# Decay tiles of an SSM loaded by one plain transfer and clamped on ScalarE, begun half a group earlier, in a hybrid attention and SSM block

## The chip, the core and the metric

The kernel runs on one core of a Trainium2 chip. The metric is the device time of one execution in microseconds; the time of a kernel is the median of its runs. The profile is taken from one further execution, whose own time stands beside its span below.

## What is computed

One layer on x (256 tokens by 2048 channels, float32): a normalised u = rms_norm(x) goes through one wide projection `w_in`; one part feeds sparse attention with an indexer, one part a Mamba-2 mixer; gates merge the two; then comes a SwiGLU channel mixer. The change touches the Mamba part, of which this is the core, and the sum over its groups:

```python
a = dt * a_head                                  # negative, per token and head
acum = cumsum(a)
decay = exp(where(causal, acum[t] - acum[s], -inf))
cb = einsum('btgn,bsgn->btsg', c, b)             # 8 groups g, state 128
y = einsum('btsg,btsgh,bsghp->btghp', cb, decay, xc)   # 8 heads h of 64 in a group
...
y = (y + d_skip * xs) * silu(z)
yg = y * rsqrt(mean(y * y) + eps) * g_norm       # mean within a group
y_ssm = sum over groups of yg @ w_ssm_branch     # 512 channels of a group each
```

The reference does this in steps of 64 tokens with a carried state. The kernel computes the whole 256 by 256 causal matrix of each head at once.

## The kernel before

Everything on the tensor engine (PE) is fp32 accuracy made of fp32r products. Weights come from memory in chunks of 1 MB, tiles `raw`, three buffers, issued on the SP queue (L415). ScalarE (ACT) rounds half a chunk to `hi` (L427), VectorE (DVE) takes the rest `lo` (L429), and PE makes three products (L489). Five pairs of `hi` and `lo` may be in flight. Some chunks are "sevens" (L440 to L455): seven block products in place of eight, for which DVE first builds the tiles `ts` from `raw` (L444, L450, L451). DVE, POOL and SP are put in order by a scheduler; the order of PE and ACT is set by hand: jobs are generators that yield a pause (a count of matmuls of the main stream, and a kind such as FREES or LATER), and between two chunk steps the jobs whose pause is over add their next piece.

The SSM stage is the loop over 8 groups at L910. For group g, `mixed()` makes 8 chunks of projection (the group's x and z, 256 by 512 each), `finish(pend...)` runs the job of group g-1 up to its result, `job_of(ssm_steps(g, ...))` starts the job of this group, and `ssm_out(g-1)` makes four chunks of `w_ssm_branch` products for the group before: its results leave PSUM through ACT as tiles `sums`, scaled by `rsg` (L900), and POOL's DMA adds them to `acc_d` in memory (L905, an accumulating transfer; 512 KB each, four per group).

The job `ssm_steps` (L803) runs beside those chunks:

- Two decay tiles `E` of 4 heads (128 by 4 by 384) are loaded by POOL: first the mask, broadcast over heads (L810), then `acum_d` (the cumulative sums, in memory), added onto it by an accumulating broadcast transfer (L812), which waits until the mask has landed.
- `cps` = C Bᵀ on PE (L819, L820), copied to `cbm` by ACT (L822).
- `conv_steps` (L727): transposes (L739), a first tap by ACT (L743), three more by DVE (L750), and one Silu of 1024 columns (L754), which waits for the job `decay_steps` (`behind`, L752).
- `decay_steps` (L789): per head two Exp with a bias per partition, 256 and 128 columns (L796); per pair of heads one DVE product with `cbm` (L800).
- Silu of z (L828); x transposed back (L835) and scaled by dt on DVE into `xdt` (L836).
- The products `yp` = xdt by E (L848), on DVE the skip (L854); z transposed (L865), product on DVE (L867), split `yh`, `yl` (L870, L873), square and sum (L878 to L886), and on POOL the small chain of the reciprocal root `rsg` (L142 to L153).

After the groups the accumulated `acc_d` is read back as two tiles `acc` of 1 MB (L960) for the attention stage, which works in four steps of 512 columns (`attn_steps`, L965).

Of the kernel before, what the change touches and what calls it, by code (L numbers as in the profile page):

```python
# [8 lines left out]
F32 = mybir.dt.float32  # L9
# [53 lines left out]
K_ID = 0  # L63
K_T = 128
K_CA = 128
K_SA = 256
K_CI = 384
K_SI = 448
K_V0 = 512
K_V1 = 640  # L70
K_N = 896


@with_exitstack
def hybrid_block(ctx, tc, xt, x, consts, mask, cols, heads, gfin, w_a, w_i, w_m, w_g, w_ab, w_sb, w_o, w_f1, w_f2, out):
    nc = tc.nc
# [51 lines left out]
    headp = cp.tile([SH, 2], F32, name="headp")  # L128
    ident = kc[:, K_ID : K_ID + P]
    neg_half = cp.tile([P, T], F32, name="neg_half")  # L130
    nc.gpsimd.memset(neg_half, -0.5)
# [143 lines left out]

    wz = cp.tile([P, 512], mybir.dt.bfloat16, name="wz")
    nc.vector.memset(wz, 0.0)
    for i in range(9):
# [317 lines left out]
    def head_steps():  # L596
# [68 lines left out]
        nc.vector.tensor_scalar(rest, dl[:, P:S], dl[:, P - 1 : P], None, ALU.add)  # L665
        nc.vector.tensor_scalar(r2, dl, -1.0, None, ALU.mult)
        nc.gpsimd.dma_start(acum_d[:, 0:P], dl[:, 0:P])
# [16 lines left out]
        tp = tr_t([P, 4, SH])  # L684
        for i, src in enumerate((r1[:, 0:P], r1[:, P:S], r2[:, 0:P], r2[:, P:S])):
            nc.tensor.transpose(tp[:, i, :], src, ident[:SH, :SH])
# [45 lines left out]
    def conv_steps(xk, cb, dst, behind=None, gap=12):  # L732

        for h in range(2):
            tp = tr_t([P, 2, S])
            for c in range(2):
                for t in range(T):
                    o = (2 * h + c) * P
                    nc.tensor.transpose(tp[:, c, t * P : (t + 1) * P], xk[t][:, o : o + P], ident)  # L739
            k = 2 * h  # L740
            for c in range(2):
                ch = cb * 4 + k + c
                nc.scalar.activation(dst[:, k + c, :], tp[:, c, :], AF.Identity, scale=ccol(C_CW, 3 * 48 + ch), bias=ccol(C_CB, ch))  # L743
# [7 lines left out]
            yield (6, FREES) if h else gap  # L751
# [32 lines left out]

    first_e = paced(v[0][0])

    acc_d = dp.tile([S, D], F32, name="acc_d")

    def decay_steps(g, Es, cbm):  # L789

        yield (6, LATER)
        for q in range(2):
            for hh in range(4):
                h = g * HPG + 4 * q + hh
                for i, e in ((2, Es[q][:, hh, 0:S]), (3, Es[q][:, hh, S:384])):
                    nc.scalar.activation(e, e, AF.Exp, bias=dcols[:, i, h : h + 1])  # L796
                yield (9, LATER)
                if hh % 2:
                    e = Es[q][:, hh - 1 : hh + 1, :]
                    nc.vector.tensor_tensor(e, e, cbm.unsqueeze(1).broadcast_to([P, 2, 384]), ALU.mult)  # L800
                    yield (3, LATER)

    def ssm_steps(g, xk, z, res):  # L803
        scaled(xk)
        Es = []
        for q in range(2):
            E = big_t([P, 4, 384], name="E")
            Es.append(E)
            with tc.issue_after(paced(xk[0]) if q else first_e) if g == 0 else nullcontext():
                nc.gpsimd.dma_start(E, mask.unsqueeze(1).broadcast_to([P, 4, 384]))  # L810
            h = g * HPG + 4 * q
            nc.gpsimd.dma_start(  # L812
                E.rearrange("p h s -> p (h s)"),
                acum_d[h : h + 4, :].rearrange("h s -> (h s)").partition_broadcast(P),
                accum_op=ALU.add,
            )
        yield 6
# [3 lines left out]
        cbm = smx.tile([P, 384], F32, tag="cbm", bufs=1, name=nm("cbm"))  # L821
        nc.scalar.activation(cbm, cps, AF.Copy)  # L822
        yield 6
        xs = mid_t([P, 4, S], name="xsc")
        decayed = job_of(decay_steps(g, Es, cbm))
        yield from conv_steps(xk, g, xs, decayed, 12 if g else 24)
        for t in range(T):
            nc.scalar.activation(z[t], z[t], AF.Silu, scale=rs(t))  # L828
        yield 12
        xdt = mid_t([P, T, 512], name="xdt")  # L830
        hs = slice(g * HPG, (g + 1) * HPG)
        for t in range(T):
# [6 lines left out]
            )  # L839
            yield 18 if t else 12  # L840
        for q in range(2):
            yp = sd_t([P, 2, S], name="yp")
# [9 lines left out]
            for m in range(2):  # L852
# [513 lines left out]
def _layout(inp):  # L1366
# [33 lines left out]
    a["consts"] = cst  # L1400
    future = np.where(np.triu(np.ones((P, P), np.float32)) > 0, 0.0, NEG_BIAS).astype(np.float32)
    a["mask"] = np.ascontiguousarray(np.concatenate([future, np.zeros((P, P), np.float32), future], axis=1))

    a["cols"] = np.ascontiguousarray(np.concatenate([
# [64 lines left out]
```

## Time and profile before

| | us |
|---|---|
| median of 3 runs | 1996.97 (1993.53 to 1997.56) |
| the profiled execution, its own time | 1997.86 |
| its span in the profile | 1995.8 |
| PE busy | 1952.8 (98%) |
| DVE busy | 1604.6 (80%) |
| ACT busy | 1177.9 (59%) |
| POOL busy | 93.2 (5%) |

The span is the time from the first to the last instruction of the profiled execution. Busy times are sums over instructions; matmuls overlap in the pipeline, so the share of PE contains some of its short waits. The mean clock granted to PE over the span was 0.994 of full speed. The SSM groups 1 to 7 lie between 230 and 860 us. There the queue of SP moved most of its bytes as weight chunks, and the queue of POOL the `sums`, the masks and `acum_d`.

### The profile page before, as it was taken

What the parts mean: (1) busy time and instruction counts of PE and PEld (TensorE: products, weight loads), DVE (VectorE), ACT (ScalarE), POOL (GpSimd) and SP (SyncE); (2) the same over time, 40 slices, a digit from 0 to 9 for tenths busy, and PEclk for the clock granted to TensorE, in tenths of its full rate; (3) what the DMA queues carried; (4) which work ended last, traced back from release to release, by engine and by line L of the source; (5) the groups of instructions that cost most, each with busy time, mean ns of one, the idle gap of its engine ahead of it and who ended that gap; (6) DMA issues with size and microseconds to landing.
All of it is one profiled execution on the core that took longest, in us unless ns stands there. A gap on an engine that the chain in (4) does not pass through costs nothing.

```text
span 1995.8 us, 23976 instructions
## 1 busy us (share of the span) xinstructions
PE 1952.8 (98%) x8990; PEld 1600.0 (80%) x8990; DVE 1604.6 (80%) x2109; ACT 1177.9 (59%) x1564; POOL 93.2 (5%) x149
## 2 busy tenths in 40 slices
PE   9999999899999999999999999999999999999998
PEld 7889787677777877778888888788888888888886
DVE  6878978777777778688998565789989999889864
ACT  6666475665765765556666445565655566555553
POOL 0000010110210210100000000000000000000000
PEclk9999999999999999999999999999999999999999
DMA  8566765957867866854455555455654655555553
GB/s 325 179 214 213 239 223 186 280 187 228 260 198 246 258 206 202 251 193 169 171 191 185 200 196 181 146 205 198 216 198 179 213 199 203 213 196 211 194 207 127
DMA packets 63908, 413.45 MB, mean 207 GB/s; under 512 B 7296, under 2 KB 7808, under 8 KB 20656
## 3 DMA queue, kind: packets, MB, share of 16 engines
q1 hardware_dynamic: 51120, 360.86, 50.1%
q0 software_dynamic: 11152, 47.29, 10.2%
q10 hardware_dynamic: 1520, 3.78, 0.5%
q8 instruction: 70, 1.15, 0.2%
q14 instruction: 46, 0.38, 0.1%
HBM read 392.93 MB, written 18.97 MB: 206 GB/s over the span
## 4 chain that ended last, share of the span: by engine, by line
PE 79%; DVE 9%; DMA 6%; ACT 4%; issue 2%; POOL 0%; SPq 0%; DVEq 0%; ACTq 0%; POOLq 0%
PE p L1199 31%; PE mm L489 29%; DMA raw<-in_w_m_dram 5%; PE mm L169 4%; PE mm L170 4%; PE mm L168 4%; DVE lo L429 4%; PE p L489 2%; ACT hi L427 1%; PE yp L848 1%; PE lg L979 1%; PE tr L1237 0%; DVE xsc L750 0%; DVE E L800 0%; DVE xb L530 0%
## 5 line engine op out<-in xcount | busy, mean ns | idle before, releaser
L489 PE MATMUL mm<-hi,ua 128*128 128x512 f32 (+1 forms) x1920 | 563.4, 394 | 2.6 <-DVE xb L530 1.5
L427 ACT ACTIVATE hi<-raw 128x1024 fp32r<-128x1024 f32 (+1 forms) x352 | 349.4, 1008 | 266.0 <-PE mm L489 161.0
L429 DVE TENSOR_TENSOR lo<-raw,hi 128x1024 fp32r<-128x1024 f32 (+1 forms) x352 | 403.5, 1161 | 120.4 <-ACT hi L427 119.7
L489 PEld LDWEIGHTS mm<-hi,ua 128*128 128x128 f32 x1920 | 354.0, 189 | 72.9 <-issue 3.0
L1121 ACT ACTIVATE hi<-raw 128x1024 fp32r<-128x1024 f32 x240 | 233.3, 979 | 132.2 <-PE p L1199 99.9
L1199 PE MATMUL p<-hi,opa 128*128 128x512 f32 x924 | 306.0, 390 | 1.5 <-ACT opf L1086 1.5
L489 PE MATMUL mm<-lo,ua 128*128 128x512 f32 (+1 forms) x960 | 301.0, 389 | 0.0
L1122 DVE TENSOR_TENSOR lo<-raw,hi 128x1024 fp32r<-128x1024 f32 x240 | 265.1, 1120 | 8.2 <-ACT hi L1121 7.4
L489 PEld LDWEIGHTS mm<-lo,ua 128*128 128x128 f32 x960 | 181.1, 189 | 37.3 <-DVE lo L429 0.3
L1199 PEld LDWEIGHTS p<-hi,opa 128*128 128x128 f32 x924 | 173.5, 188 | 37.6 <-ACT opf L1086 2.0
L200 DVE TENSOR_TENSOR lo<-raw,hi 128x1024 fp32r<-128x1024 f32 (+2 forms) x97 | 115.1, 1194 | 85.3 <-ACT hi L199 85.2
L1199 PE MATMUL p<-lo,opa 128*128 128x512 f32 x462 | 180.2, 391 | 0.0
L199 ACT ACTIVATE hi<-raw 128x1024 fp32r<-128x1024 f32 (+2 forms) x97 | 99.6, 1035 | 110.2 <-PE mm L170 98.4
L1199 PE MATMUL p<-hi,act 128*128 128x512 f32 x416 | 133.1, 390 | 0.0
L1199 PE MATMUL p<-hi,opb 128*128 128x512 f32 x352 | 126.9, 390 | 0.0
L1199 PEld LDWEIGHTS p<-lo,opa 128*128 128x128 f32 x462 | 86.7, 188 | 17.9 <-DVE lo L1122 0.2
L1121 ACT ACTIVATE hi<-tb 128x1024 fp32r<-128x1024 f32 x45 | 47.8, 1062 | 87.6 <-PE p L1199 45.1
L427 ACT ACTIVATE hi<-ts 128x1024 fp32r<-128x1024 f32 (+1 forms) x64 | 65.7, 1042 | 45.8 <-DVE ts L451 24.9
L1199 PEld LDWEIGHTS p<-hi,act 128*128 128x128 f32 x416 | 78.1, 188 | 16.3
L489 PE MATMUL mm<-hi,yh 128*128 128x512 f32 x256 | 86.4, 410 | 3.6 <-ACT sums L900 2.7
L1199 PE MATMUL p<-lo,act 128*128 128x512 f32 x208 | 80.5, 390 | 0.0
L489 PE MATMUL mm<-lo,yh 128*128 128x512 f32 x256 | 79.5, 391 | 0.0
(335 smaller groups left out, 3232.8 us busy)
## 6 DMA issues: line engine op xcount, KB each, us to landing
raw<-in_w_f_dram SPq DMA_DIRECT2D x132, 1024.0 KB, 4.8
raw<-in_w_m_dram SPq DMA_DIRECT2D x120, 1024.0 KB, 5.4
raw<-in_w_sb_dram SPq DMA_DIRECT2D x32, 1024.0 KB, 5.0
acc_d<-sums POOLq DMA_DIRECT2D x32, 512.0 KB, 10.0
raw<-in_w_g_dram SPq DMA_DIRECT2D x16, 1024.0 KB, 4.8
raw<-in_w_ab_dram SPq DMA_DIRECT2D x16, 1024.0 KB, 4.8
raw<-in_w_o_dram SPq DMA_DIRECT2D x16, 1024.0 KB, 4.8
E<-in_mask_dram POOLq DMA_DIRECT2D x16, 768.0 KB, 9.6
```

Source lines behind the costliest of these rows:

```text
L168: nc.tensor.matmul(o, lh, rh, start=(kt == 0), stop=False)
L169: nc.tensor.matmul(o, lh, rl, start=False, stop=False)
L170: nc.tensor.matmul(o, ll, rh, start=False, stop=(kt == nk - 1))
L199: hi_ops.append(nc.scalar.activation(hi[:, o], src[:, o], AF.Copy))
L200: nc.vector.tensor_tensor(lo[:, o], src[:, o], hi[:, o].bitcast(F32), ALU.subtract)
L427: nc.scalar.activation(hi, src, AF.Copy)
L429: lows.append(lambda: nc.vector.tensor_tensor(lo, src, hi.bitcast(F32), ALU.subtract))
L489: nc.tensor.matmul(ps[c], x, b[part], start=c in begun, stop=left[c] == 0)
L848: nc.tensor.matmul(yp[64 * c : 64 * c + 64, m, k * P :], xdt[:, k, h * 64 : (h + 1) * 64], Es[q][:, hh, lo : lo + n], start=(k == 0), stop ...
L1121: nc.scalar.activation(hi, src, AF.Copy)
L1122: nc.vector.tensor_tensor(lo, src, hi.bitcast(F32), ALU.subtract)
L1199: nc.tensor.matmul(ps[i], x, y, start=start and j == 0, stop=left[i] == 0)
```

## The change

1. `consts` gets a tile `tri` (128 by 128, ones on and above the diagonal), and the input `mask` goes. `dcols` rows 2 and 3 hold the plus cumulative sums, so one DVE product (64 by 256) goes.
2. An `E` tile is loaded by one plain broadcast transfer of `acum_d`; the mask load and the accumulation go.
3. Per head, ACT now computes Relu(dcol - E) in place, in the same two pieces of 256 and 128 columns (16 per group); per pair of heads one Exp(-E) of 768 columns follows (4 per group, new). The clamp keeps the exponent at or below zero, and the causal zeros come from `cbm`, whose two diagonal blocks of 128 columns DVE now multiplies by `tri` (16 in all, new); ACT copies only the 128 columns between them.
4. The decay of group g+1 is a job of its own that starts right behind the `yp` products of group g (`decay(g + 1)`), with its loads; `finish(decayed)` stands just ahead of `yp`. The Silu of the convolution no longer waits for the decays.
5. Pauses are set anew: 12 for 6 in the convolution, 9 with FREES ahead of the Silu of z, `9 if g else 48` behind it, 18 for 6 in the rounds of the top-k search.
6. `acc` is read back in quarters: eight transfers of 256 KB, the first pair at the place of the old ones, the others behind POOL copies that pace them by the projections of the attention steps.
7. The zero tile `wz` of the warm-up moves into the buffer `rtmp`.

The core of the diff:

```diff
-    def decay_steps(g, Es, cbm):
-        yield (6, LATER)
-        for q in range(2):
-            for hh in range(4):
-                h = g * HPG + 4 * q + hh
-                for i, e in ((2, Es[q][:, hh, 0:S]), (3, Es[q][:, hh, S:384])):
-                    nc.scalar.activation(e, e, AF.Exp, bias=dcols[:, i, h : h + 1])
-                yield (9, LATER)
-                if hh % 2:
-                    e = Es[q][:, hh - 1 : hh + 1, :]
-                    nc.vector.tensor_tensor(e, e, cbm..., ALU.mult)
-                    yield (3, LATER)
+    def decay_steps(g, Es):
         for q in range(2):
             E = big_t([P, 4, 384], name="E")
             Es.append(E)
-                nc.gpsimd.dma_start(E, mask.unsqueeze(1).broadcast_to([P, 4, 384]))
-            nc.gpsimd.dma_start(E..., acum_d[h : h + 4, :]...partition_broadcast(P), accum_op=ALU.add)
+                nc.gpsimd.dma_start(E..., acum_d[h : h + 4, :]...partition_broadcast(P))
         yield 6
         cps = tr_t([P, 384])
...
-        nc.scalar.activation(cbm, cps, AF.Copy)
+        nc.scalar.activation(cbm[:, P:S], cps[:, P:S], AF.Copy)
+        for lo in (0, S):
+            nc.vector.tensor_tensor(cbm[:, lo : lo + P], cps[:, lo : lo + P], tri, ALU.mult)
+        yield (18 if g else 6, LATER)
+        for q in range(2):
+            for hh in range(4):
+                h = g * HPG + 4 * q + hh
+                for i, e in ((2, Es[q][:, hh, 0:S]), (3, Es[q][:, hh, S:384])):
+                    nc.scalar.activation(e, e, AF.Relu, scale=-1.0, bias=dcols[:, i, h : h + 1])
+                yield (6, LATER)
+                if hh % 2:
+                    e = Es[q][:, hh - 1 : hh + 1, :]
+                    nc.scalar.activation(e, e, AF.Exp, scale=-1.0)
+                    nc.vector.tensor_tensor(e, e, cbm..., ALU.mult)
+                    yield (6, LATER)
...
-        decayed = job_of(decay_steps(g, Es, cbm))
-        yield from conv_steps(xk, g, xs, decayed, 12 if g else 24)
+        yield from conv_steps(xk, g, xs, None, 12 if g else 24)
+        yield (9, FREES)
         for t in range(T):
             nc.scalar.activation(z[t], z[t], AF.Silu, scale=rs(t))
-        yield 12
+        yield 9 if g else 48
...
+        Es, decayed = decays.pop(g)
+        finish(decayed)
         for q in range(2):
             yp = sd_t([P, 2, S], name="yp")
...
+        if g + 1 < GROUPS:
+            decay(g + 1)
...
-    for t in range(T):
-        nc.gpsimd.dma_start(acc[t], acc_d[t * P : (t + 1) * P, :])
+    def load_acc(j):
+        c = slice(j * 512, (j + 1) * 512)
+        for t in range(T):
+            nc.gpsimd.dma_start(acc[t][:, c], acc_d[t * P : (t + 1) * P, c])
+
+    load_acc(0)
     for j in range(NKV):
         v = mixed()
+        if j + 1 < NKV:
+            with tc.issue_after(paced(v[0][0])):
+                load_acc(j + 1)
```

How this moves instructions is seen at two places. The first is POOL beside `ssm_out`, in one steady group. Before (the number behind a tile's name tells tiles apart; in brackets, whom the instruction waits for):

```order
L905 DMA acc_d<-sums_4309 128x1024 [waits Activation_49] x2
L810 DMA E_4910<-in_mask_dram 128x4x384 [waits PE_49]
L810 DMA E_4913<-in_mask_dram 128x4x384 [waits DMASW4_49,DMASW7_49,DMASW3_49,DMASW1_49]
L905 DMA acc_d<-sums_4444 128x1024 [waits Activation_49]
L812 DMA E_4910<-acum_d 128x1536 [waits DMASW5_49,DMASW0_49]
L905 DMA acc_d<-sums_4444 128x1024 [waits Activation_49]
L812 DMA E_4913<-acum_d 128x1536 [waits DMASW6_49,DMASW2_49]
```

And now, where L799 is the plain load and L920 the write of `sums`:

```order
L920 DMA acc_d<-sums_4370 128x1024 [waits Activation_49] x2
L799 DMA E_4640<-acum_d 128x1536 [waits DMASW7_49,DMASW0_49,PE_49]
L799 DMA E_4642<-acum_d 128x1536 [waits DMASW2_49,DMASW1_49,PE_49]
L920 DMA acc_d<-sums_4477 128x1024 [waits DMASW5_49,Activation_49]
L920 DMA acc_d<-sums_4477 128x1024 [waits DMASW6_49,Activation_49]
```

The two loads have taken the places of the two masks, and the second pair of transfers, behind the `sums` of the second half, is gone. The tiles E_4640 and E_4642 belong to the group after the one whose `yp` follows here.

The second place is ACT, from the last Exp of a group to the Silu of its convolution (`xsc`), the same group as in the first fence. Before:

```order
L796 ACTIVATE E_4913<-E_4913,dcols 128x256
L796 ACTIVATE E_4913<-E_4913,dcols 128x128
L427 ACTIVATE hi_5195<-raw_5043 128x512 [waits PE_49,Activation_49]
L754 ACT_TABLE_LOAD
L754 ACTIVATE xsc_4939<-xsc_4939 128x1024
L828 ACTIVATE xb_4666<-xb_4666,rstd 128x512 x2
L427 ACTIVATE hi_5218<-raw_5089 128x1024 [waits DMAHW1_49,DVE_49,PE_49]
L427 ACTIVATE hi_5231<-ts_5215 128x1024 [waits DVE_49,PE_49]
```

And now, at the Silu of a steady group (L915 is the `sums` copy, L430 the `hi`, L839 the Silu of z):

```order
L915 ACTIVATE sums_4981<-mm_5004,rsg_4892 128x512
L915 ACTIVATE sums_4981<-mm_5005,rsg_4892 128x512
L756 ACT_TABLE_LOAD [waits DVE_49]
L756 ACTIVATE xsc_4996<-xsc_4996 128x1024 [waits Activation_49]
L839 ACTIVATE xb_4736<-xb_4736,rstd 128x512 x2
L430 ACTIVATE hi_5113<-raw_4974 128x1024 [waits PE_49]
L430 ACTIVATE hi_5123<-raw_5031 128x1024 [waits DMAHW7_49,PE_49]
L915 ACTIVATE sums_5088<-mm_5089,rsg_4892 128x512 [waits PE_49]
```

The Silu stands between the two halves of `ssm_out` and no longer behind the last Exp. The decays of that group (16 Relu, one table load, 4 Exp) were done ahead of it, among the `hi` of the second half of the projection chunks:

```order
L815 ACTIVATE E_4640<-E_4640,dcols 128x256
L815 ACTIVATE E_4640<-E_4640,dcols 128x128
L430 ACTIVATE hi_4848<-raw_4754 128x1024 [waits PE_49]
L819 ACT_TABLE_LOAD
L819 ACTIVATE E_4640<-E_4640 128x768 [waits Activation_49]
L815 ACTIVATE E_4640<-E_4640,dcols 128x256
L815 ACTIVATE E_4640<-E_4640,dcols 128x128
L430 ACTIVATE hi_4871<-raw_4777 128x1024 [waits DMAHW2_49,PE_49]
```

A table load stands ahead of the first Exp of a group as before; in group 0 two more are there than before, since its decays lie among the Silus of the convolutions. On PE the `yp` products of a steady group stand right behind `ssm_out`, in the first two chunks of the next projection; before, they stood further back among its sevens.

## Rows read from the trace of the kernel before

**Rows 1.** The page, part 1: busy time, share of the span and number of instructions of the engines.

```profile
PE 1952.8 (98%) x8990; PEld 1600.0 (80%) x8990; DVE 1604.6 (80%) x2109; ACT 1177.9 (59%) x1564; POOL 93.2 (5%) x149
```

**Rows 2.** The waits of PE in the stretch 230 to 860 us, which holds SSM groups 1 to 7: who waited, for whom, us in total, times, longest.

```profile
PE yp L848 <- DVE xdt L836: 15.0, 6, 4.4
PE mm L489 <- ACT sums L900: 2.7, 2, 2.1
PE sqp L886 <- DVE ysq L882: 2.1, 1, 2.1
```

**Rows 3.** The timeline of PE around the `yp` products of five groups: start, us, engine, line, what, in brackets the idle time before it and its releaser.

```profile
394.49 1.98 PE L848 MATMUL yp<-E,xdt 128*64 128x128 f32 x12 [4.43 <-DVE xdt L836]
...
472.41 1.97 PE L848 MATMUL yp<-E,xdt 128*64 128x128 f32 x12 [2.84 <-DVE xdt L836]
...
550.16 1.97 PE L848 MATMUL yp<-E,xdt 128*64 128x128 f32 x12 [2.34 <-DVE xdt L836]
...
701.93 1.09 PE L848 MATMUL yp<-E,xdt 128*64 128x128 f32 x12 [2.63 <-DVE xdt L836]
...
773.86 1.52 PE L848 MATMUL yp<-E,xdt 128*64 128x256 f32 x16
```

**Rows 4.** The chain of work in the stretch 420 to 500 us, around the `yp` of one group: start, us, what. A DMA's piece runs from its issue to its landing.

```profile
457.02 11.18 DMA raw<-in_w_m_dram
...
469.40 2.36 DVE lo L429 x2
471.76 0.61 DVE xdt L836
...
472.41 1.97 PE yp L848 x12
474.39 4.86 PE mm L489 x12
...
480.70 2.99 PE mm L489 x12
```

**Rows 5.** Busy time by stretch of 5 us: PE, PEld, DVE, ACT, POOL, then the clock that PE was granted (1.00 is 2.4 GHz, 0.50 is 1.2 GHz), the busy share of the DMA engines and GB/s.

```profile
390.00:395.00 5.00, 0.57 (x8) 0.51 (x8) 3.53 (x4) 4.00 (x4) 0.00 (x0) 0.81 0.69 236
395.00:400.00 5.00, 5.00 (x19) 3.55 (x16) 2.49 (x4) 0.00 (x0) 0.00 (x0) 0.50 0.91 339
470.00:475.00 5.00, 2.59 (x14) 1.78 (x15) 3.89 (x5) 2.31 (x3) 0.00 (x0) 0.66 0.93 352
475.00:480.00 5.00, 5.00 (x22) 3.69 (x22) 1.61 (x3) 0.71 (x1) 0.00 (x0) 0.65 0.78 287
550.00:555.00 5.00, 4.84 (x22) 3.56 (x23) 3.25 (x5) 2.00 (x2) 0.00 (x0) 0.66 0.76 261
```

**Rows 6.** DMA issues in the stretch 240 to 860 us: what, how many, KB each, median us from issue to landing.

```profile
raw<-in_w_m_dram SPq DMA_DIRECT2D x68, 1024.0 KB, 7.5
...
acc_d<-sums POOLq DMA_DIRECT2D x32, 512.0 KB, 10.0
E<-in_mask_dram POOLq DMA_DIRECT2D x12, 768.0 KB, 10.3
E<-acum_d POOLq DMA_DIRECT2D x12, 768.0 KB, 16.7
```

**Rows 7.** DMA in the stretch 425 to 472 us, the loaded part of one group: for the two large queues packets, MB, and the share of 16 engines' time that the packets took; then the weight loads of the stretch with their median us to landing.

```profile
q0 software_dynamic: 1248, 5.24, 50.8%
q1 hardware_dynamic: 1052, 7.70, 43.0%
...
raw<-in_w_m_dram SPq DMA_DIRECT2D x6, 1024.0 KB, 9.8
```

**Rows 8.** The same view of 430 to 440 us, beside which writes of sums (issued at 428 and 431) and one mask load were under way.

```profile
raw<-in_w_m_dram SPq DMA_DIRECT2D x2, 1024.0 KB, 8.6
```

**Rows 9.** The page, part 6: the weight loads of the FFN, with no other large transfer beside them.

```profile
raw<-in_w_f_dram SPq DMA_DIRECT2D x132, 1024.0 KB, 4.8
```

**Rows 10.** Groups of ACT instructions by form, whole run: line, operation, out<-in, count, busy us, mean ns of one, idle before.

```profile
L796 ACT ACTIVATE E<-E,dcols 128x256 f32<-128x256 f32 x64 | 32.2, 503 | 0.1
...
L796 ACT ACTIVATE E<-E,dcols 128x128 f32<-128x128 f32 x64 | 25.2, 394 | 0.0
...
L427 ACT ACTIVATE hi<-raw 128x768 fp32r<-128x768 f32 x14 | 11.5, 842 | 9.0 <-PE mm L489 4.7 <-DMA raw<-in_w_i_dram 3.9 <-ACT hi L427 0.4
...
L796 ACT ACT_TABLE_LOAD x8 | 10.3, 1283 | 0.1
```

**Rows 11.** Groups of DVE instructions by form, 240 to 860 us, with the same columns.

```profile
L800 DVE TENSOR_TENSOR E<-E,cbm 128x768 f32<-128x768 f32 x28 | 26.7, 954 | 5.8 <-ACT E L796 5.8
...
L750 DVE SCALAR_TENSOR_TENSOR xsc<-tr,colp,xsc 128x254 f32<-128x254 f32 x28 | 12.4, 473 | 0.0
...
L591 DVE SCALAR_TENSOR_TENSOR isc<-relu,widx,isc 128x128 f32<-128x128 f32 x12 | 4.2, 348 | 0.8 <-ACT relu L586 0.7
```

**Rows 12.** The waits of ACT, 245 to 860 us: for whom, us, times, longest.

```profile
ACT hi L427 <- PE mm L489: 98.7, 86, 6.5
ACT hi L427 <- DMA raw<-in_w_m_dram: 60.0, 18, 6.6
```

**Rows 13.** Busy time in two stretches around group 0, columns as in group 5.

```profile
159.00:192.00 33.00, 33.00 (x186) 31.77 (x185) 28.46 (x45) 23.20 (x40) 2.54 (x3) 1.00 0.63 202
195.00:225.00 30.00, 27.77 (x138) 22.28 (x137) 30.00 (x49) 15.72 (x18) 3.31 (x4) 1.00 0.69 219
```

More of the change, by code (lines that the diff above doesn't have):

```diff
@@ L63, with hybrid_block @@
 K_ID = 0
[L64 to L71, printed above, removed]
+K_TRI = 128
+K_T = 256
+K_CA = 256
+K_SA = 384
+K_CI = 512
+K_SI = 576
+K_V0 = 640
+K_V1 = 768
+K_N = 1024
 @with_exitstack
-def hybrid_block(ctx, tc, xt, x, consts, mask, cols, heads, gfin, w_a, w_i, w_m, w_g, w_ab, w_sb, w_o, w_f1, w_f2, out):
+def hybrid_block(ctx, tc, xt, x, consts, cols, heads, gfin, w_a, w_i, w_m, w_g, w_ab, w_sb, w_o, w_f1, w_f2, out):
     nc = tc.nc
@@ L129, in hybrid_block @@
     ident = kc[:, K_ID : K_ID + P]
+    tri = kc[:, K_TRI : K_TRI + P]
     neg_half = cp.tile([P, T], F32, name="neg_half")
@@ L274, in lhs_quads @@
         return f
-    wz = cp.tile([P, 512], mybir.dt.bfloat16, name="wz")
-    nc.vector.memset(wz, 0.0)
+    wzf = smx.tile([P, 512], F32, tag="rtmp", name="wz")[:, :256]
+    nc.vector.memset(wzf, 0.0)
+    wz = wzf.bitcast(mybir.dt.bfloat16)
     for i in range(9):
@@ L684, in head_steps @@
         tp = tr_t([P, 4, SH])
-        for i, src in enumerate((r1[:, 0:P], r1[:, P:S], r2[:, 0:P], r2[:, P:S])):
+        for i, src in enumerate((r1[:, 0:P], r1[:, P:S], dl[:, 0:P], dl[:, P:S])):
             nc.tensor.transpose(tp[:, i, :], src, ident[:SH, :SH])
@@ L717, in index_steps @@
                 nc.vector.match_replace(isc[t], m8, isc[t], NEG_SEL)
-                yield (6, LATER)
+                yield (18, LATER)
             nc.vector.tensor_scalar(isc[t], isc[t], -3.2e38, NEG_BIAS, ALU.is_gt, ALU.mult)
@@ L785, in hybrid_block @@
     first_e = paced(v[0][0])
+    first_x = []
     acc_d = dp.tile([S, D], F32, name="acc_d")
-    def decay_steps(g, Es, cbm):
-        yield (6, LATER)
-        for q in range(2):
-            for hh in range(4):
-                h = g * HPG + 4 * q + hh
-                for i, e in ((2, Es[q][:, hh, 0:S]), (3, Es[q][:, hh, S:384])):
-                    nc.scalar.activation(e, e, AF.Exp, bias=dcols[:, i, h : h + 1])
-                yield (9, LATER)
-                if hh % 2:
-                    e = Es[q][:, hh - 1 : hh + 1, :]
-                    nc.vector.tensor_tensor(e, e, cbm.unsqueeze(1).broadcast_to([P, 2, 384]), ALU.mult)
-                    yield (3, LATER)
-    def ssm_steps(g, xk, z, res):
-        scaled(xk)
-        Es = []
+    def decay_steps(g, Es):
         for q in range(2):
@@ L808, in ssm_steps @@
             Es.append(E)
-            with tc.issue_after(paced(xk[0]) if q else first_e) if g == 0 else nullcontext():
-                nc.gpsimd.dma_start(E, mask.unsqueeze(1).broadcast_to([P, 4, 384]))
[L811 to L816, printed above, removed]
+            with tc.issue_after(paced(first_x[0]) if q else first_e) if g == 0 else nullcontext():
+                h = g * HPG + 4 * q
+                nc.gpsimd.dma_start(
+                    E.rearrange("p h s -> p (h s)"), acum_d[h : h + 4, :].rearrange("h s -> (h s)").partition_broadcast(P)
+                )
         yield 6
@@ L821, in ssm_steps, with decay @@
         cbm = smx.tile([P, 384], F32, tag="cbm", bufs=1, name=nm("cbm"))
-        nc.scalar.activation(cbm, cps, AF.Copy)
-        yield 6
+        nc.scalar.activation(cbm[:, P:S], cps[:, P:S], AF.Copy)
[11 more added lines that the diff above has]
+                    nc.scalar.activation(e, e, AF.Exp, scale=-1.0)
+                    nc.vector.tensor_tensor(e, e, cbm.unsqueeze(1).broadcast_to([P, 2, 384]), ALU.mult)
+                    yield (6, LATER)
+    decays = {}
+    def decay(g):
+        Es = []
+        decays[g] = Es, job_of(decay_steps(g, Es))
+    def ssm_steps(g, xk, z, res):
+        scaled(xk)
+        if g == 0:
+            first_x.append(xk[0])
+            decay(0)
+        yield 12
         xs = mid_t([P, 4, S], name="xsc")
-        decayed = job_of(decay_steps(g, Es, cbm))
-        yield from conv_steps(xk, g, xs, decayed, 12 if g else 24)
+        yield from conv_steps(xk, g, xs, None, 12 if g else 24)
+        yield (9, FREES)
         for t in range(T):
             nc.scalar.activation(z[t], z[t], AF.Silu, scale=rs(t))
-        yield 12
+        yield 9 if g else 48
         xdt = mid_t([P, T, 512], name="xdt")
@@ L1389, in _layout @@
     cst[:, K_ID : K_ID + P] = np.eye(P, dtype=np.float32)
+    cst[:, K_TRI : K_TRI + P] = np.triu(np.ones((P, P), np.float32))
     for dim, cb, sb in ((HD, K_CA, K_SA), (IDX, K_CI, K_SI)):
@@ L1400, in _layout @@
     a["consts"] = cst
-    future = np.where(np.triu(np.ones((P, P), np.float32)) > 0, 0.0, NEG_BIAS).astype(np.float32)
-    a["mask"] = np.ascontiguousarray(np.concatenate([future, np.zeros((P, P), np.float32), future], axis=1))
     a["cols"] = np.ascontiguousarray(np.concatenate([
```

4 lines of the change are left out of this document (1 added, 3 removed).

## The prediction

> **What bounds the kernel now.** I read the busy shares first: PE 98%, DVE 80%, ACT 59%, POOL 5% [rows 1]. So only what makes PE wait, or slows its clock, can be won or lost; work taken from ACT or POOL pays only where PE waits for it in the end. Then the waits of PE in the stretch of groups 1 to 7 [rows 2]: 15.0 us in six pieces ahead of `yp`, for `xdt`; 2.7 us for a `sums` bank; 2.1 us ahead of `sqp`. The timeline shows the first three large pieces, 4.43, 2.84 and 2.34 us, a later one of 2.63, and a last group that has none [rows 3]; its 16 products there run straight on. That group is the one in which no tiles of a next group are loaded.
>
> Next, what ends last there. The chain around one `yp` runs back from `xdt` over two `lo` to a weight chunk that took 11.18 us from issue to landing [rows 4]. DVE does `xdt` in its queue behind the `lo` of that chunk, so late weights delay `xdt`, not the decays. Undisturbed, such a chunk lands in 4.8 us [rows 9]; beside the writes of `sums` and one mask load in 8.6 [rows 8]; the median of the loaded 47 us is 9.8 [rows 7]. The POOL transfers beside it are `sums` (10.0 us), masks (10.3) and the accumulating `acum_d` (16.7) [rows 6].
>
> Last, the clock. After three of the waits the granted clock fell to the lower level (0.50 in the five us from 395, about 0.66 from 470, 475 and 550) [rows 5]. The same 12 `yp` products took 1.97 to 1.98 us there against 1.09 at full clock [rows 3], the next 12 matmuls 4.86 against 2.99 [rows 4]. Over the five stretches, counting only what fell in PE's own work (a quarter of a us in the first, 1.3 of 1.7 in the third, the whole shortfall in the others), this is 0.25 + 2.5 + 1.3 + 1.75 + 1.7 = 7.5 us.
>
> **The change, part by part.** *Transfers.* In the loaded 47 us POOL's queue takes 50.8% of 16 engines, 23.9 us for 5.24 MB; SP's 43.0%, 20.2 us for 7.70 MB, 2.62 us a MB [rows 7]. Of the 5.24 MB two masks and two `acum_d` loads of 768 KB are 1.57 each. Without masks, and with `acum_d` at SP's price (1.57 by 2.62, 4.1 us) or still at its share (7.2 us), 13.7 to 16.8 us are left: 7 to 10 us of engine time saved per group. More than that, the loads now stand where the masks stood, beside the `sums`, and nothing is behind the second half's `sums`, where the late chunk of [rows 4] was in flight. The second load still waits on POOL for the first half's `sums` to land, with the second half's behind it, as the second mask did: no new wait.
>
> *yp.* In [rows 4] the chunk landed after 11.18 us and `yp` waited 2.84 [rows 3], so 8.3 would have done. What a chunk takes beside a plain `acum_d` load no row shows. Bounds: 4.8 alone [rows 9] and 9.8, the median with everything [rows 7]; I take 8.6, the row with `sums` and one plain mask load, which is the nearest [rows 8]. So 0.3 us too late, 0.4 with spread: the 15.0 us become some 0.4 in each of 7 groups, 2.8. Waits that short should leave the clock alone, as the 2.63 us one did [rows 3]: its 7.5 us come back too.
>
> The Trainium skill, page "DMA: Bandwidth & Descriptors", section "Queues, rings and completion order", says that each DMA engine takes turns between queues packet by packet. The trace agrees: a packet takes about 307 ns in either queue (43.0% of 47 us on 16 engines over 1052 packets, 50.8% over 1248), and a chunk takes 9.8 us, twice its 4.8. By that rule a plain load slows a chunk nearly as much as an accumulating one while it lasts, and only ends sooner: at 2.62 us a MB a packet of 6 KB is some 257 ns by my estimate, so 4.8 by (307 + 257) / 307 is 8.8 us, and the residue 0.5 a group for 0.4. That is the first rival if it holds at the place that counts.
>
> *Order.* `yp` comes about half a projection earlier, and the Silu of the convolution no longer stands behind 16 Exp. `rsg` and `ysq` then have more time before PE asks for them: the 2.7 and 2.1 us [rows 2] go. Below that I see nothing; late next would be `xdt` itself, behind transposes, Silu and table load.
>
> *ACT.* The 16 Relu have the shapes of the 16 Exp they replace, 503 and 394 ns [rows 10]: no change. New are 4 Exp of 768 columns a group; nearest is a 768-column copy, 842 ns [rows 10], so 3.4 us a group, 27 in all. Two more table loads in group 0 are 2.6 us. ACT waited 98.7 us for PE and 60.0 for weights in these stretches [rows 12]: in groups 1 to 7 these cover it. If the cover were gone, each group would cost 3.4. In group 0 ACT was busy 23.2 us of 33 with PE at 33.00 [rows 13]; 3.4 + 2.6 on top leaves 4 us of slack in sum, but in bursts. Its cost lies between 0 and the whole 6.0; I take 1.5, nearer to nothing since 10 us of idle are there.
>
> *DVE.* 16 products of 128 columns, at 348 ns [rows 11], are 5.6 us over the run, under waits of DVE for weights and ACT. The four `E` products a group (954 ns) only move earlier. In group 0 DVE is busy 30.00 of 30 us from 195 on [rows 13]; there 3 of them move ahead, against `cbm`'s 0.7: nothing or a small gain.
>
> *The rest.* `acc` in quarters moves the same bytes later, with three more tiny POOL copies; POOL is 5% busy [rows 1]. If the first quarter were late, the first attention step's product waits, behind PE work of its own. 64 KB more of constants, one DVE product less and the pauses of the top-k: nothing, to within half a us.
>
> **Sum.** 15.0 + 7.5 + 2.7 + 2.1 = 27.3 us gained, less 2.8 and 1.5: 23.0. The profiled execution took 1997.86; that gives 1974.9. The median is 0.9 below that execution, so **1974.0**. The forecast's own range is 1967 (no residue and group 0 free, 1969.7, and 3 `E` products of 0.95 us taken out of group 0's full DVE) to 1981 (residue 1 us a group, 4.2 more, and 3 more in group 0).
>
> **Rivals.** *Waits only shrink.* Four writes of `sums` of 512 KB a group stay as accumulations, and plain loads take turns with the weights too. If half of the waits and of the dips stay: 1997.9 - 7.5 - 3.75 - 4.8 + 1.5 - 0.9 = 1982.4. For it: DMA engines at 0.93 at 470 [rows 5]; against: the late chunk flew beside what is now gone.
>
> *ACT becomes the bound (slower).* `finish(decayed)` stands ahead of `yp`, and every group's 16 Relu, 4 Exp and 4 DVE products must be through. If the new Exp and the switch of tables fall on the path, 3.4 + 1.28 us in each of 7 groups are 32.8, and with dips as before (7.5) the waits cost 40.3 in place of 22.5: 1997.9 + 17.8 - 4.8 + 1.5 - 0.9 = 2011.5. It decides from a wait of (22.5 + 4.8 - 1.5) / 7 = 3.7 us a group without dips, 2.6 with them. For it: they stand between the `hi` that PE needs, and what is left of them when `yp` is due goes ahead of the next `hi`, so PE would wait for both. Against: ACT's 59% and its 158.7 us of waits [rows 1, 12]. The Trainium skill, page "ScalarE: Activation LUTs", section "Rules for kernel authors", would put a relu on VectorE. By rows, the two pieces on DVE would be near 473 + 348 ns a head [rows 11] against 503 + 394 [rows 10], 0.6 us a group less in sum, but on the queue that `xdt` stands in; so I give the rule no more than this rival's chance.
>
> *It doesn't do what it says.* The loads wait on POOL until the `sums` ahead have landed, as the masks did; if they came as late as the old ones, `yp` would wait for the decays as long as for `xdt`, and only 4.8 - 1.5 us are won: 1993.7.
>
> **How the numbers follow.** A measurement tells some 0.2%, 4 us, from no change. Forecast 0.62; waits only shrink 0.24; ACT as the bound 0.08; not earlier 0.06. Faster: the first two, 0.86. Slower: ACT, 0.08, and 0.01 of the last, for a costlier group 0 (6.0 us in place of 1.5); same 0.05. The range goes from 3 us below the best case, for waits too short to be listed, to the first rival with three quarters of the waits and dips left, 5.6 us above its half, and 2 us of group 0: 1964 to 1990.
>
> **What would show it.** Right: the waits of PE list `yp` with under 4 us, no stretch of 5 us in groups 1 to 7 with a clock below 0.9, weight chunks of the groups at a median under 7.5, ACT busy about 1207 (1177.9 + 27 + 2.6), no wait for `sums` or `ysq`. Wrong: `yp` waiting for `E`, chunks still at 10 beside the plain loads, or a PE wait for `hi` in group 0 over 3 us.

## The result: 1967.31 us, 1.5% faster than before

| | before | after |
|---|---|---|
| median | 1997.26 (1993.53 to 1999.06, 4 runs) | 1967.31 (1966.91 to 1968.28, 4 runs) |
| profiled execution, its span | 1997.86, 1995.8 | 1967.47, 1965.5 |

The ratio is 0.9853, 95% interval 0.9836 to 0.987. The profile after, part 1 of its page, against [rows 1]:

```profile
PE 1942.8 (99%) x8990; PEld 1598.6 (81%) x8990; DVE 1608.6 (82%) x2124; ACT 1206.7 (61%) x1598; POOL 86.4 (4%) x142
```

ACT has 28.8 us more of work (29.6 were forecast), PE 10.0 less. The waits of PE from 230 to 860 us, against [rows 2]:

```profile
PE mm L492 <- DVE xb L533: 1.5, 1, 1.5
PE tr L741 <- ACT xa L731: 0.6, 2, 0.3
```

None of the three waits of before is left. The wait for `xb` is an old one that stood at 865 us, outside that stretch. The `yp` products of one group, on the timeline of PE, against [rows 3]; neither row has a wait:

```profile
360.28 1.52 PE L861 MATMUL yp<-E,xdt 128*64 128x256 f32 x16
...
364.67 1.52 PE L861 MATMUL yp<-E,xdt 128*64 128x256 f32 x16
```

DMA issues from 240 to 860 us, against [rows 6], with the median us to landing last:

```profile
raw<-in_w_m_dram SPq DMA_DIRECT2D x74, 1024.0 KB, 4.9
...
acc_d<-sums POOLq DMA_DIRECT2D x32, 512.0 KB, 8.2
E<-acum_d POOLq DMA_DIRECT2D x12, 768.0 KB, 7.2
```

The median weight chunk lands in 4.9 us, where 7.5 was the median before. That median is of all chunks, and most of them now fly with no load beside them. Those issued from 418 to 445 us, where two loads and four `sums` were under way, lie between that and the 8.6 that the prediction took beside a load:

```profile
raw<-in_w_m_dram SPq DMA_DIRECT2D x4, 1024.0 KB, 6.8
```

No 5 us of groups 1 to 7 have a granted clock under 0.97. The ACT groups by form, whole run, against [rows 10] (mean ns behind the busy us):

```profile
L815 ACT ACTIVATE E<-E,dcols 128x256 f32<-128x256 f32 x64 | 31.6, 494 | 0.0
...
L819 ACT ACTIVATE E<-E 128x768 f32<-128x768 f32 x32 | 26.9, 839 | 0.4
```

A Relu costs what the Exp cost, and a 768-column Exp 839 ns for the 842 taken. Something was lost in group 0; stretches of 10 us, columns as in [rows 5]:

```profile
200.00:210.00 10.00, 8.42 (x39) 6.38 (x37) 9.40 (x15) 5.35 (x6) 0.00 (x0) 0.92 0.57 204
210.00:220.00 10.00, 10.00 (x60) 7.14 (x59) 10.00 (x20) 1.11 (x2) 1.08 (x2) 0.91 0.83 270
```

Behind a wait of 1.17 us for a `lo` at 206 us the clock is 0.92 and 0.91, which is some 1.7 us lost; before, it was 1.00 there. The wait for `xb` stands at 865.63 us before and at 832.52 after: 33.1 us had been won by then, of which 2.8 were lost again up to the end of the span, in stages that the change does not touch.

### The profile page after: what moved, and what is told of

The parts are those of the page before. It is cut to its first block, busy times and chain, and to the rows that moved or that the text cites. A ratio compares the mean times of both kernels' runs of the same rounds, so it can differ in the third digit from the quotient of the medians.

```text
span 1965.5 us, 23995 instructions
## 1 busy us (share of the span) xinstructions
PE 1942.8 (99%) x8990; PEld 1598.6 (81%) x8990; DVE 1608.6 (82%) x2124; ACT 1206.7 (61%) x1598; POOL 86.4 (4%) x142
## 3 DMA queue, kind: packets, MB, share of 16 engines
q8 instruction: 70, 1.15, 0.2%
## 5 line engine op out<-in xcount | busy, mean ns | idle before, releaser
L430 ACT ACTIVATE hi<-raw 128x1024 fp32r<-128x1024 f32 (+1 forms) x352 | 351.5, 1008 | 183.6 <-PE mm L492 138.9
L430 ACT ACTIVATE hi<-ts 128x1024 fp32r<-128x1024 f32 (+1 forms) x64 | 66.6, 1046 | 85.2 <-DVE ts L454 32.2
L432 DVE TENSOR_TENSOR lo<-ts,hi 128x1024 fp32r<-128x1024 f32 (+1 forms) x64 | 76.6, 1205 | 23.6 <-ACT hi L430 21.8
L492 PE MATMUL mm<-hi,yh 128*128 128x512 f32 x256 | 82.1, 402 | 0.0
L1161 DVE TENSOR_TENSOR ta<-raw 128x1024 f32<-128x1024 f32 x45 | 55.1, 1224 | 32.8 <-DMA raw<-in_w_f_dram 32.6
```

Of the source, the lines that this page charges most:

```text
L430: nc.scalar.activation(hi, src, AF.Copy)
L432: lows.append(lambda: nc.vector.tensor_tensor(lo, src, hi.bitcast(F32), ALU.subtract))
L492: nc.tensor.matmul(ps[c], x, b[part], start=c in begun, stop=left[c] == 0)
L1161: nc.vector.tensor_tensor(ta, raw[:, 2:4, :], raw[:, 1:3, :], ALU.subtract)
```

## The experiments

Four parts of the change are taken apart here: how `E` is loaded, the clamp (Relu, Exp of 768, triangle), when the decays start, and the pauses. In this table each kernel's median stands beside its ratio to the kernel before, which was timed again beside it (medians 1994.4 to 1997.3). The kernels with the clamp also have the quarters of `acc` and the other small parts of the change. In the row "plain, clamp" two further pauses are shorter than in the rows below it, 6 for 18 ahead of the Relu and 6 for 12 ahead of the convolution. The early start and the new pauses without the clamp were not run.

| kernel | loads of E | clamp | decays start | pauses | us | ratio, 95% |
|---|---|---|---|---|---|---|
| before | mask + accumulate | no | late | old | 1997.26 | |
| plain alone | plain | no | late | old | 1974.14 | 0.9864 to 0.9911 |
| plain, clamp | plain | yes | late | old | 2003.14 | 1.0019 to 1.0044 |
| ... and pauses | plain | yes | late | new | 1990.95 | 0.9965 to 0.9997 |
| ... or early | plain | yes | early | old | 1999.38 | 1.0005 to 1.0038 |
| the change | plain | yes | early | new | 1967.31 | 0.9836 to 0.987 |
| its old loads | mask + accumulate | yes | early | new | 1978.9 | 0.9893 to 0.9943 |

**Plain loads in the old kernel.**

```diff
-   nc.gpsimd.dma_start(E, mask.unsqueeze(1).broadcast_to([P, 4, 384]))
-   nc.gpsimd.dma_start(E..., acum_d[h : h + 4, :]..., accum_op=ALU.add)
+   nc.gpsimd.dma_start(E..., acum_d[h : h + 4, :]...)
-   nc.scalar.activation(e, e, AF.Exp, bias=dcols[:, i, h : h + 1])
+   nc.scalar.activation(e, e, AF.Exp, bias=dcols[:, i - 2, h : h + 1])
```

> The kernel before with one plain load of acum_d per E tile and neither mask nor accumulation; order, pauses and every instruction of the engines stay. The causal mask is left out and the Exp take another bias, so the values are not the reference's. Theory T (late weight chunks alone made yp wait): chunk landings at about 5 us, no wait of yp for xdt, no dip of the clock, 1972 to 1980; the waits for sums and ysq (4.8 us) stay. Theory C (coupled: each part moves the wait to the next tight place of the same chain, and only all together remove it): landings at 5 us too, but PE then waits elsewhere in the group, for sums or late lo, and the time is 1981 to 1994.

It took 1974.14 us. The waits of PE from 180 to 870 us, and the DMA issues from 240 to 860:

```profile
PE sqp L883 <- DVE ysq L879: 2.1, 1, 2.1
PE mm L489 <- ACT sums L897: 2.0, 1, 2.0
PE yp L845 <- DVE xdt L833: 1.8, 2, 1.5
```

```profile
raw<-in_w_m_dram SPq DMA_DIRECT2D x72, 1024.0 KB, 6.5
```

Of the 1.8 us for `yp` 1.5 are group 0's; in the other groups it hardly waits. The two waits that the prediction put on the order stand as before. The chunk that [rows 4] follows, which took 11.18 us, now takes 7.2:

```profile
raw<-in_w_m_dram SPq DMA_DIRECT2D x1, 1024.0 KB, 7.2
```

PE and ACT have the same instructions in the same order as before; on DVE one `lo` in each of five groups moved ahead of the first of the two `xdt`, and the second, for which `yp` had waited, stands behind the same `lo` as before. Earlier landing of `E` is not the cause, since ACT waits for an `E` in neither trace. So late weight chunks had made `yp` wait: theory T holds in the old order, and 23 us are the 15.0 and 7.5 of the sum. Two of its details missed: the median chunk takes 6.5 us and not 5, and one dip is left (0.93 and 0.73 from 340 to 350 us, behind the wait of 2.0 us for `sums`). Mask and accumulation went together here; which of them made the chunks late in the old order was not tested.

**Old loads in the new kernel.**

```diff
-   nc.gpsimd.dma_start(E..., acum_d[h : h + 4, :]...)
+   nc.gpsimd.dma_start(E, mask...)            # zeros
+   nc.gpsimd.dma_start(E..., acum_d[h : h + 4, :]..., accum_op=ALU.add)
```

> The changed kernel with the old pair of loads per E tile: a plain broadcast of a mask (all zeros here) and acum_d added onto it by an accumulating transfer. Everything else, the early start of the decays included, stays. Theory T (transfers: the waits ahead of yp were late weight chunks, and they went because masks and accumulating loads no longer fly beside the chunk that xdt stands behind): the median landing of the w_m chunks between 240 and 860 us goes from 4.9 back to 7 us or more, the waits of yp for xdt come back at 1.5 to 3 us a group, some with a dip of the clock, and the time is 1982 to 1992. Theory O (order: they went because the decays and the Silu left the path to xdt, and yp moved): landings get worse, PE does not care, 1967 to 1972.

1978.9 us, between the two, 11.6 above the change. `yp` does not wait, and the chunks' median is 5.8. PE waits elsewhere, from 180 to 870 us:

```profile
PE mm L492 <- DVE xa L533: 4.5, 5, 1.4
PE tr L806 <- DVE xa L533: 1.8, 1, 1.8
```

The second of these is a `cps`. Near 180 us there is a wait of 1.5 us for a `hi`, and behind it the clock is 0.71 and 0.61 (180 to 190 us), 3.4 us lost. The next run tells bytes from accumulation.

**Two plain loads in the new kernel**, the first a zero mask that the second overwrites:

```diff
+   nc.gpsimd.dma_start(E, mask...)            # zeros
    nc.gpsimd.dma_start(E..., acum_d[h : h + 4, :]...)
```

> The changed kernel with a second plain load ahead of each E load (a zero mask, overwritten by it): the bytes and the places on POOL of the kernel with early decays and accumulating loads (1978.9), but no accumulation in SBUF. If the bytes and the chain of two loads make its loss: 1977 to 1981. If it is the accumulation: 1967 to 1971. By packets taking turns, the bytes are some two thirds of it: 1973 to 1977.

1966.01 us, with the bytes of the run before and the same instruction order on every engine. DMA beside the loads of one group, first with accumulation from 436 to 470 us, then with two plain loads from 430 to 464, since that kernel is 5.9 us ahead at this place; with each, the landing of one chunk, the same in both, issued at 450 us and at 444:

```profile
q0 software_dynamic: 833, 3.61, 48.0%
...
raw<-in_w_m_dram SPq DMA_DIRECT2D x1, 1024.0 KB, 11.4
```

```profile
q0 software_dynamic: 825, 3.58, 37.8%
...
raw<-in_w_m_dram SPq DMA_DIRECT2D x1, 1024.0 KB, 8.9
```

POOL's queue moves nearly the same bytes in both, but with accumulation they hold the engines for 48.0% of the 34 us, without for 37.8%. In the change itself, with one plain load, the same chunk took 5.9 us:

```profile
raw<-in_w_m_dram SPq DMA_DIRECT2D x1, 1024.0 KB, 5.9
```

In the four other groups from 370 to 660 us this chunk took 4.8 us with one plain load, 6.1 to 7.2 with two, and 10.0 to 11.0 with accumulation. So the second load's bytes do slow it, by 1.4 to 3.0 us, and accumulation by another 2.6 to 4.2. The `hi` on ACT shows what follows, again first with accumulation:

```profile
461.63 2.01 ACT L430 ACTIVATE hi<-raw 128x1024 fp32r<-128x1024 f32 x2 [2.93 <-DMA raw<-in_w_m_dram]
```

```profile
453.20 2.24 ACT L430 ACTIVATE hi<-raw 128x1024 fp32r<-128x1024 f32 x2 [0.37 <-DMA raw<-in_w_m_dram]
```

Both lines are the same two `hi`; with accumulation they wait 2.93 us for that chunk (the bracket that ends the line), without 0.37. So the bytes alone stay within the slack of the chunk and cost nothing that shows (1966.0 against 1967.3), and the accumulation on top of them costs 12.9 us. Of these 3.4 are the lower clock near 180 us, which is not there with two plain loads; most of the rest are the waits for `xa` and `cps`. Accumulation without the bytes of a second load was not run.

**The clamp in the old order**: late start, Silu behind the decays, old pauses (the excerpt shows the late start and two of the pauses; the others stand under "Old pauses" below).

```diff
-       yield (18 if g else 6, LATER)              # ahead of the Relu
+       yield (6, LATER)
...
+       decay(g)                                   # in ssm_steps, for every g
-       yield 12                                   # ahead of the convolution
+       yield 6
...
-       yield from conv_steps(xk, g, xs, None, 12 if g else 24)
+       yield from conv_steps(xk, g, xs, decays[g][1], 12 if g else 24)
...
-       if g + 1 < GROUPS:
-           decay(g + 1)
```

> The changed kernel with both the late start of the decays (Silu behind them) and the old pauses: in effect the old order with plain loads, 16 Relu, 4 Exp of 768 columns and the triangle on DVE. Its values are right. Beside the old kernel with plain loads alone (1974.1) it tells what the clamp costs in the old order. If ACT covers it there: 1973 to 1977. If 3.4 us more of ACT a group fall on the way to the Silu and xdt: 6 groups by up to 3.4, 1984 to 1995, waits of yp for xdt in the list again.

2003.14 us, 29.0 above the old order with plain loads alone, and above both ranges of the expectation. The waits of PE from 180 to 870 us:

```profile
PE tr L845 <- ACT xsc L756: 14.5, 8, 3.1
PE mm L492 <- ACT sums L912: 12.5, 12, 1.9
```

ACT around one group's Silu, and the two waits of PE there:

```profile
517.30 0.85 ACT L819 ACTIVATE E<-E 128x768 f32<-128x768 f32 x1
518.05 1.25 ACT L912 ACTIVATE sums<-mm,rsg 128x512 f32<-128x512 f32 x2
519.19 1.06 ACT L430 ACTIVATE hi<-raw 128x1024 fp32r<-128x1024 f32 x1
520.27 1.28 ACT L756 ACT_TABLE_LOAD   x1
521.57 1.06 ACT L756 ACTIVATE xsc<-xsc 128x1024 f32<-128x1024 f32 x1
```

```profile
522.68 0.66 PE L845 MATMUL tr<-kc,xsc 128*128 128x128 f32 x4 [1.31 <-ACT xsc L756]
...
525.42 1.07 PE L492 MATMUL mm<-hi,ua 128*128 128x512 f32 x2 [0.70 <-ACT sums L912]
```

ACT goes from the last Exp over `sums` and `hi` to the table load and the Silu without a gap, and PE stands 1.31 us for that Silu and 0.70 for `sums`. The expectation named `yp`; the wait came two steps earlier in the same chain. This is the rival that makes ACT the bound, at some 4 us a group.

**Late start, new pauses**: the late start of the edit above, with all pauses of the change.

> The changed kernel with the decays of a group started at the start of its own job again and the Silu of the convolution behind them, as before; plain loads, Relu, Exp of 768 columns and the new pauses stay. Theory T: chunks still land at about 5 us, yp waits at most 0.5 us a group: 1968 to 1974. Theory O: yp waits 2 us or more a group, 1982 to 1995, since Silu and xdt are again behind 16 Relu and now 4 more Exp.

1990.95 us, with chunks landing in 4.9 us:

```profile
PE mm L492 <- ACT sums L913: 11.4, 10, 2.0
```

```profile
427.47 1.22 PE L492 MATMUL mm<-hi,yh 128*128 128x512 f32 x2 [1.48 <-ACT sums L913]
...
502.75 1.07 PE L492 MATMUL mm<-hi,yh 128*128 128x512 f32 x2 [1.48 <-ACT sums L913]
```

```profile
425.00:430.00 5.00, 3.45 (x11) 2.24 (x10) 4.10 (x7) 4.97 (x11) 1.43 (x2) 0.83 0.61 153
430.00:435.00 5.00, 5.00 (x20) 4.00 (x20) 4.03 (x5) 4.52 (x9) 0.00 (x0) 0.83 1.04 256
500.00:505.00 5.00, 3.45 (x14) 2.33 (x13) 4.10 (x7) 4.97 (x10) 1.43 (x2) 1.00 0.58 136
```

Neither theory holds as written. The chunks are early and `yp` does not wait, as T has it, but its 1968 to 1974 is missed; the time falls in O's range, though not for `yp`: ACT, busy 4.97 of 5 us from 425, is late with the `sums`. Five groups have a wait of 1.48 us for them. Behind the one at 427 us the clock fell to 0.83 in two stretches, behind the one at 502 it did not, and behind the three that follow it fell again. From 230 to 865 us the clock costs 8.6 us of the 23.6 by which this kernel is slower than the change.

**Old pauses.** First all of those below, then those of the steady groups, then those of the start.

```diff
-           yield (12, FREES) if h else gap            # steady
+           yield (6, FREES) if h else gap
-       yield (9, FREES)                               # steady
-       yield 9 if g else 48                           # 9: steady, 48: start
+       yield 12
-               yield (18, LATER)                      # top-k: start
+               yield (6, LATER)
```

> The changed kernel with the old pauses: 6 in place of 12 behind the second half of the convolution, no pause ahead of the Silu of z, 12 behind it, 6 in the top-k rounds. If the pauses only follow the new order: 1967 to 1970. If they carry the part of the gain that stood in the waits for sums, ysq and in group 0: 1972 or more, with those waits in the list again.

> The changed kernel with only the pauses of the steady groups as before: 6 behind the second half of the convolution, none ahead of the Silu of z, 12 behind it; group 0 keeps its 48 and the top-k its 18. From the kernel with all old pauses, whose steady groups lost 1.0 us before the transposes of xsc, 0.9 before the sums and 1.2 at a late lo: 3 us in each of 7 groups, 1984 to 1990. If the loss came from group 0 and the top-k: 1968 to 1973.

> The changed kernel with only the pauses of the start as before: 12 in place of 48 behind the Silu of z in group 0, and 6 in place of 18 in the top-k rounds. From the kernel with all old pauses, which lost 5.3 us in group 0 before the transposes of xsc and 2.7 us with a dip of the clock at 234: 1974 to 1981. If the start does not matter: 1967 to 1970.

1999.38, 1992.75 (0.997 to 1.0003) and 1973.11 us (0.9855 to 0.991). The waits of PE from 180 to 870 us with the steady groups' old pauses:

```profile
PE tr L845 <- ACT xsc L756: 8.1, 7, 3.1
PE p L492 <- DVE lo L432: 5.7, 6, 1.0
PE mm L492 <- ACT sums L914: 3.5, 5, 0.7
```

With those of the start, the waits from 180 to 240 us, and the clock:

```profile
PE p L492 <- ACT hi L430: 2.9, 1, 2.9
PE tr L846 <- ACT xsc L756: 2.0, 1, 2.0
```

```profile
230.00:235.00 5.00, 3.04 (x6) 2.11 (x7) 4.57 (x5) 5.00 (x8) 0.00 (x0) 0.50 0.35 146
```

Of the 32 us some 25 are lost by the steady groups' set alone, a little more than expected. By the times of the same products in both traces only 1.3 of them lie ahead of 242 us, so this is 3 us or more a group. The Silu follows closely on the taps: in five groups PE waits 0.9 us for `xsc`, 0.7 for `sums` and 1.0 for a `lo`; in one group `xsc` is waited for 3.1 us, with the clock at 0.80 and 0.52 behind it. The pauses of the convolution and of the Silu of z are shorter in group 0 too in this run. 5.8 us are the start, just under what was expected, with a dip to 0.50; the 48 of group 0 and the 18 of the top-k were set back together, so they are not told apart.

**One more ACT instruction per pair of heads.**

```diff
                    nc.scalar.activation(e, e, AF.Exp, scale=-1.0)
+                   nc.scalar.activation(e, e, AF.Copy)
```

> The changed kernel with one more ACT instruction of 768 columns (a copy in place) behind each Exp of a pair: 4 a group, some 3.0 us of ACT a group more, at the place of the new Exp. If ACT has room there: 1967 to 1970. If the new Exp already fill it: 3.0 us in each of 7 groups, 1980 to 1990, with PE waiting for hi or for yp.

1998.51 us (1.0002 to 1.003): 31 us more than the change, well above the expectation, for 25.5 us more of ACT in eight groups (1232.2 busy against 1206.7). The waits of PE from 180 to 870 us:

```profile
PE tr L741 <- ACT xa L731: 18.6, 11, 2.8
```

```profile
494.13 0.82 ACT L819 ACTIVATE E<-E 128x768 f32<-128x768 f32 x1
494.99 0.84 ACT L820 ACTIVATE E<-E 128x768 f32<-128x768 f32 x1
495.74 1.04 ACT L430 ACTIVATE hi<-raw 128x1024 fp32r<-128x1024 f32 x1
496.68 1.32 ACT L731 ACTIVATE xa<-xa,rstd 128x512 f32<-128x512 f32 x2
```

```profile
497.44 0.33 PE L741 MATMUL tr<-kc,xa 128*128 128x128 f32 x1 [2.52 <-ACT xa L731]
```

The second row of ACT is the added copy; behind it and a `hi` stands the scaling of the next group's x, `xa`, and PE waits for that. In seven groups this is 18.6 us, and the clock fell behind several of these waits (0.65 to 0.67 in the stretches from 420, 570 and 575), 11.9 us in sum from 230 to 865 us; together these are nearly all of the 31. ACT has no room left in that place.

**The clamp on VectorE.**

```diff
-   nc.scalar.activation(e, e, AF.Relu, scale=-1.0, bias=dcols[:, i, h : h + 1])
+   nc.vector.tensor_scalar(e, e, dcols[:, i, h : h + 1], 0.0, ALU.subtract, ALU.min)
-   nc.scalar.activation(e, e, AF.Exp, scale=-1.0)
+   nc.scalar.activation(e, e, AF.Exp)
```

> The changed kernel with the clamp on VectorE: min(E - dcol, 0) in place of the 16 Relu of a group, Exp without the minus sign. ACT loses some 7 us a group, DVE gains 16 operations of 256 and 128 columns, at the nearest rows up to 6.6 us a group. If ACT is the tighter of the two between the sums and yp, 1964 to 1967; if DVE is, since xdt and lo stand in its queue, 1970 to 1985.

1975.15 us (0.9869 to 0.9918). DVE groups by form:

```profile
L815 DVE TENSOR_SCALAR E<-E,dcols 128x256 f32<-128x256 f32 x64 | 22.2, 347 | 3.8 <-DMA E<-acum_d 2.8 <-issue 0.9
...
L815 DVE TENSOR_SCALAR E<-E,dcols 128x128 f32<-128x128 f32 x64 | 17.9, 280 | 0.0
```

DVE does it in 347 and 280 ns, ACT took 494 and 388. In the steady groups PE waits no more than 0.6 us at a time, so they hardly change; the loss, 7.8 us, lies nearly all ahead of 230 us, in six waits of 0.9 to 1.7 us.

**acc whole, and a later rotation.**

```diff
-   load_acc(0) ... load_acc(j + 1)                    # first kernel
+   nc.gpsimd.dma_start(acc[t], acc_d[t * P : (t + 1) * P, :])
...
+       if j == 0:                                     # second kernel, in attn_steps
+           yield 24
```

> The changed kernel with acc read back whole, two transfers of 1 MB at the old place. The quarters were costed at nothing: 1966 to 1969. If the burst delays weight chunks at the start of the attention stage, 1969 to 1974, with a wait of PE for lo near 800 us.

> The changed kernel with a pause of 24 ahead of the first attention step, so that DVE builds the tiles ts of the next chunk (L453, L454) and part of xb ahead of the rotation of the queries. It aims at the longest wait of PE that is left, 1.5 us at 832 us for xb (L533), which stands in DVE's queue behind that rotation. If it removes it: 1965.5 to 1966.5. If the wait only moves by the same DVE work: 1967 to 1968.

The first took 1970.45 us (0.984 to 0.9893; its runs 1967.37 to 1971.93), 3 us above the change or near nothing by its fastest run. Its waits of PE from 780 to 860 us:

```profile
PE mm L492 <- DVE xb L533: 1.6, 1, 1.6
PE mm L492 <- DVE xa L533: 1.1, 1, 1.1
```

The second of these is new, and the clock is 0.91 and 0.75 from 830 to 840 us, another 1.7 us; whether the quarters carry 3 us its spread leaves open. The later rotation took 1965.88 us (0.9828 to 0.9869), 1.4 us below the change and not clear of it. The wait for `xb` shrank only from 1.5 to 1.2 us.

## Why the prediction was right, and which step was not

- *The signs.* Those named for right all came: `yp` is not among the waits, no stretch of groups 1 to 7 has a clock below 0.9, chunks land in 4.9 us, ACT is busy 1206.7, and nothing waits for `sums` or `ysq`. Those for wrong did not.
- *Late weights made `yp` wait, and the clock followed.* Shown: plain loads alone bring 1974.1, the 22.5 us of those two terms. The residue of 0.4 us a group did not come: the prediction had 8.3 us as enough for the chunk ahead of `xdt` and took 8.6, and with plain loads alone it took 7.2.
- *`sums` and `ysq`, 4.8 us.* Gone in the change, still there with plain loads alone. The change stands 6.8 us below that kernel, which is what is left of larger terms in both directions (below).
- *ACT: "in groups 1 to 7 these cover it".* This is the step that failed. ACT's waits [rows 12] are a sum over the stretch, not room at the place where the Exp are added. In the old order the clamp costs 29.0 us, of the 37.5 by which the slower rival stood above the forecast (2011.5 against 1974.0); it becomes free only through the early start and the pauses together, 35.8 us for both, where the pauses alone bring 12.2 and the early start alone 3.8. And then ACT is full: 0.8 us more per pair costs 31 us.
- *The pauses.* The prediction put those of the top-k at "nothing, to within half a us" and gave the others no price. Set back, those of the steady groups cost 25.4 us and those of the start, the top-k's among them, 5.8. That the total came out near is luck in this part: the new order and the pauses pay for what the clamp takes, the sum had neither the 29.0 us nor the 35.8, and they nearly cancel.
- *"Waits that short should leave the clock alone".* The waits of 0.4 us that this was said of did not come, so it stays untested. The reason given, the 2.63 us wait of before [rows 3], does not carry it: waits of 1.48 us were followed by a lower clock in four of five groups of the late start with new pauses, and one of 1.17 us in group 0 of the change. Length alone does not tell.
- *Transfers taking turns.* By the rule of the Trainium skill, page "DMA: Bandwidth & Descriptors", section "Queues, rings and completion order", each engine takes turns between queues packet by packet. The trace agrees that bytes beside a chunk slow it (5.9 to 8.9 us in the group shown). My estimate from it, that a second plain load costs two thirds of what the old pair costs (1973 to 1977 us), failed: the run took 1966.0, since the work behind that chunk had this much slack. The first rival, that waits only shrink, is out: with plain loads, in either order, `yp` hardly waits from group 1 on.
- *Relu on VectorE.* The Trainium skill's page "ScalarE: Activation LUTs", section "Rules for kernel authors", advises it. The operation is faster there in the rows above, the kernel 7.8 us slower, with the loss around group 0, where DVE is full [rows 13].
- *Group 0, 1.5 us.* The size agrees, a dip of 1.7 us and waits of PE that differ little from those before, but the cause is not shown. With two plain loads the same wait for a `lo` (1.15 us) came with no dip.
- *Size.* 29.9 us against 23.0. Of the difference 2.8 are the residue that did not come, some 1.5 are waits of 0.3 to 0.6 us in the trace of before that the sum left out (at 236, 297 and 831 us), and 1.1 are clock, since the whole shortfall in the five stretches of [rows 5] is 8.6 us and the sum took 7.5 of it. Against them 2.8 us were given back behind 832 us. The rest no run settles.

## What to carry to other kernels

A sum of idle time says nothing of room at one place: put one extra instruction of the planned length there and see what it costs. In an order that is written by hand, pauses are part of any change of length, and one that replaces a load by arithmetic may need a new place and new pauses together. What a transfer costs here is told by the one chunk that the bound engine will stand for: see how late that chunk may land, and then what flies beside it.

## What the runs showed of the hardware

An accumulating broadcast of 768 KB into SBUF behind a plain one took 14.0 us in the median (240 to 860 us) where a plain one behind a plain one took 11.1; the weight chunks had 5.8 against 5.0, and the kernel 12.9 us more with the same order of instructions. For nearly the same bytes in 34 us (3.61 and 3.58 MB) POOL's queue held the DMA engines for 48.0% of the time with accumulation and for 37.8% without. The same wait of 1.48 us was followed by a clock of 0.83 in one group and left it at 1.00 in the next.
